# One unit for a differential head's context tiles, and the first latent leading products moved into the last head

## Chip, cores, metric

One Trainium2 chip, one of its cores. The metric is the device time of the whole program in microseconds (us).

## What is computed

Two layers over 1024 latent tokens and 256 context tokens of width 1024. The even layer projects the tokens and runs two groups of attention heads side by side; the odd layer runs an mLSTM and a neighbourhood attention. The change touches the attention of the even layer, for the latent tokens (keys: latent and context, 1280) and for the context tokens (keys: context alone, 256):

```python
def diff_attention(q1, q2, k1, k2, v, lam):
    def one(a, b_):
        s1 = jnp.einsum('bhqd,bhkd->bhqk', a, k1).astype(F32) * DA_SCALE
        s2 = jnp.einsum('bhqd,bhkd->bhqk', b_, k2).astype(F32) * DA_SCALE
        p = jax.nn.softmax(s1, axis=-1) - lam * jax.nn.softmax(s2, axis=-1)
        return jnp.einsum('bhqk,bhkd->bhqd', p.astype(v.dtype), v)
    return blocked_queries(one, q1, q2)

def softmax_attention(q, k, v, scale):
    def one(qb):
        s = jnp.einsum('bhqd,bhkd->bhqk', qb, k).astype(F32) * scale
        p = jax.nn.softmax(s, axis=-1).astype(v.dtype)
        return jnp.einsum('bhqk,bhkd->bhqd', p, v)
    return blocked_queries(one, q)
```

There are 4 differential heads (two maps each) and 8 latent (MLA) heads, which the kernel takes in 4 pairs. After the differential product comes an RMS norm and a gate.

## The kernel before

The program is a chain of stages: projections of layer 0, the attention stage, an output product with layer norm, and the same for layer 1. Only the attention stage is touched. It goes over four `Differential` units (the heads, `da`) and then four `Latent` units (the pairs, `mla`). A token tile is 128 queries: tiles 0 to 7 are latent tokens, 8 and 9 context tokens (`LT` is 8).

**A differential tile** (`Differential.plan`, line 554). For each of its two maps b, TensorE multiplies the queries with the keys' high and low parts into a score tile `s` of three PSUM banks (L565, L566; six matmuls for 1280 keys), VectorE takes the negated row maximum (`top`, L1227), ScalarE the exponential with its row sum (L1234), and then the score tile is free. VectorE combines the two maps with a ratio (L579, L580, L585), TensorE turns the result in groups of four (L1251), ScalarE and VectorE copy it out of PSUM (L518), TensorE multiplies it with the values (L596). ScalarE keeps the product (L600) and sums its squares (L605). After tiles 3, 7 and 9, `finish` (L629) normalizes, turns (L655), gates (L660) and stores (L665) a group of tiles.

There are **two score tiles** (`s`, 2 x 3 banks) and two turning tiles (`tp`, one bank each), which is all of PSUM. A map of a context tile has 256 keys only, and takes a score tile, a maximum and an exponential of its own all the same.

**A latent pair** works on blocks of keys by queries, with the keys in the partitions, in three one-bank tiles `st` (L760 to L762). So that its exponentials need no maximum in that layout, each query's shift is made beforehand: `Latent.shifts` (L702) gives a list of steps, one for each head a of the pair and each tile i of a group of four (or two) query tiles. A step is a rough score product in an `s` tile (L713) and its negated maximum (`nmx`, L721); after a group's last step the maxima are turned into a row (L729) and put beneath the queries (L734). A pair has three groups: tiles 0 to 3, tiles 4 to 7 (eight steps each) and the context tiles 8 and 9 (four steps). While one group's blocks run, the steps of the next group are interleaved with them.

**Order.** The instructions' order on each engine is fixed when the program is built. `Plan.add` (L428 ff.) lists tasks with an engine, an estimated cost, what they come after and which buffers they take and give. `Plan.run` (L463) looks at the first 99 tasks that are left, and emits the one that could start first by those estimates, with a small correction for each kind of task. Each engine then works through its instructions strictly in that order; a waiting instruction holds up all behind it. The main loop lists, for each head, the tiles in the order 0, 1, 2, 8, 3, 4, 9, 5, 6, 7, and the loads of the next head (`loaded`, which come into the place of the head before this one) at tile 4. After the last head it lists the eight steps of the first latent group, and then a task `banks`, which takes both score tiles at once, gives one back and makes the three `st` tiles out of the other's banks. Latent blocks can only follow `banks`.

## Time and profile before

| | |
|---|---|
| three runs | 1952.52, 1952.61, 1955.57 us (median 1952.61) |
| the profiled execution | 1954.08 us, span 1952.4 us, mean granted TensorE clock 0.966 |
| busy, share of the span | TensorE (PE) 93%, weight loads (PEld) 77%, VectorE (DVE) 57%, ScalarE (ACT) 37%, GpSimd (POOL) 27% |
| differential heads | from 460 us to 708.7 us |
| latent pairs | first block at 743.3 us, to about 1035 us |

The profile comes from one execution, times are from the start of its span. TensorE's busy time is that of pipelined matmuls whose ends are modelled, and TensorE's sequencer pairs each matmul with a weight load; an fp32 product shows as two matmuls. PEclk is the clock that was granted, as a share of full speed. A wait is put down to what ended it.

### The profile page before, as it was taken

To read this page: it belongs to the slowest core of one execution; us is meant where nothing else is said; L and a number is where in the kernel's file an instruction comes from. 1 tells how busy PE (TensorE), PEld (TensorE's weight loads), DVE (VectorE), ACT (ScalarE), POOL (GpSimd) and SP (SyncE) were. 2 spreads that over 40 slices of the span, in tenths; PEclk is the share of its full clock that TensorE was granted. 3 is DMA by queue.
4 is the path that set the end of the run, shared out by engine and by line. 5 is a ranking of instruction groups with operands and counts; after the bars stand their busy time and mean duration, and the time that the engine had idled before them with its cause. 6 is when DMAs were issued, how large, how long until landed. Compare 5 with 4: busy or idle time off the path is not lost.

```text
span 1952.4 us, 29575 instructions
## 1 busy us (share of the span) xinstructions
PE 1807.2 (93%) x11069; PEld 1508.0 (77%) x11069; DVE 1118.1 (57%) x2155; ACT 722.3 (37%) x1432; POOL 527.4 (27%) x542
## 2 busy tenths in 40 slices
PE   7999999999888889898899989999998998998898
PEld 5898998887777775555556779888898877877686
DVE  3654124314878887656666864665776324666756
ACT  2311014434665554343452312233553224444521
POOL 1433233100102212354463431220111002223444
PEclk9999999999989998898899999999999999999999
DMA  9756424677534644504016333224543366676652
GB/s 281 236 202 219 159 75 127 191 204 187 128 76 115 170 100 135 128 6 116 25 60 213 130 108 117 73 83 159 162 128 93 101 187 177 163 206 188 177 162 86
DMA packets 241588, 275.95 MB, mean 141 GB/s; under 512 B 25042, under 2 KB 201118, under 8 KB 241446
## 3 DMA queue, kind: packets, MB, share of 16 engines
q1 hardware_dynamic: 241446, 274.07, 48.6%
q8 instruction: 87, 1.43, 0.3%
q14 instruction: 55, 0.45, 0.1%
HBM read 193.14 MB, written 87.16 MB: 144 GB/s over the span
## 4 chain that ended last, share of the span: by engine, by line
PE 59%; DVE 13%; DMA 4%; issue 2%; ACT 2%; POOL 1%; SPq 1%; DVEq 0%; POOLq 0%; ACTq 0%
PE mm L390 6%; PE mm L392 6%; PE mm L391 6%; PE tp L796 4%; PE tp L596 3%; DVE nm L1227 3%; PE mm L1876 3%; PE mm L1877 2%; PE mm L1878 2%; PE st L760 2%; PE st L762 2%; PE st L761 2%; PE s L713 2%; DVE nmx L721 2%; PE tp L2309 2%
## 5 line engine op out<-in xcount | busy, mean ns | idle before, releaser
L347 POOL TENSOR_TENSOR wlo<-raw,whi 128x1024 fp32r<-128x1024 f32 (+2 forms) x39 | 94.4, 2420 | 227.2 <-ACT whi L339 223.9
L390 PE MATMUL mm<-whi,hhi 128*128 128x256 f32 (+1 forms) x496 | 147.8, 298 | 0.0
L392 PE MATMUL mm<-whi,hlo 128*128 128x256 f32 (+1 forms) x496 | 146.9, 296 | 0.2 <-DVE hlo L290 0.2
L391 PE MATMUL mm<-wlo,hhi 128*128 128x256 f32 (+1 forms) x496 | 146.6, 296 | 0.0
L1227 DVE TENSOR_REDUCE nm<-s 128x1 f32<-128x1280 f32 (+1 forms) x80 | 100.8, 1274 | 59.1 <-PE s L566 58.1
L339 ACT CAST whi<-raw 128x1024 fp32r<-128x1024 f32 (+2 forms) x54 | 56.0, 1036 | 180.8 <-DMA raw<-in_ev_w_in_dram 71.2
L721 DVE TENSOR_REDUCE nmx<-s 128x1 f32<-128x1280 f32 (+1 forms) x80 | 100.6, 1271 | 38.6 <-PE s L713 38.3
L2266 POOL TENSOR_SCALAR np<-np,nrz 128x640 f32<-128x640 f32 x64 | 53.0, 831 | 232.3 <-DVE nrz L2263 211.3
L565 PE MATMUL s<-o 128*128 128x512 f32 (+1 forms) x208 | 85.5, 417 | 27.4 <-ACT p L1234 27.1
L1234 ACT ACTIVATE p<-s,nm 128x1280 f32<-128x1280 f32 (+1 forms) x80 | 92.6, 1158 | 39.1 <-DVE nm L1227 31.4
L390 PEld LDWEIGHTS mm<-whi,hhi 128*128 128x128 f32 x496 | 94.8, 191 | 2.1 <-issue 1.7
L392 PEld LDWEIGHTS mm<-whi,hlo 128*128 128x128 f32 x496 | 94.8, 191 | 0.5 <-DVE hlo L290 0.4
L391 PEld LDWEIGHTS mm<-wlo,hhi 128*128 128x128 f32 x496 | 94.9, 191 | 0.2
L596 PE MATMUL tp<-v,pt 128*128 128x128 f32 x672 | 82.0, 280 | 0.3
L596 PEld LDWEIGHTS tp<-v,pt 128*128 128x128 f32 x672 | 80.4, 196 | 2.2 <-ACT pt L518 1.0
L1876 PE MATMUL mm<-h,whi 128*128 128x512 f32 x192 | 78.9, 411 | 3.3 <-DVE hv L1912 3.3
L713 PE MATMUL s<-o 96*128 96x512 f32 (+1 forms) x208 | 64.0, 410 | 17.0 <-DVE nmx L721 15.7
L776 ACT ACTIVATE pt<-st 128x512 f32<-128x512 f32 (+1 forms) x88 | 50.8, 578 | 72.3 <-PE st L762 67.8
L1877 PE MATMUL mm<-h,whi 128*128 128x512 f32 x192 | 76.3, 397 | 0.0
L1878 PE MATMUL mm<-h,wlo 128*128 128x512 f32 x192 | 76.1, 396 | 0.0
L644 POOL TENSOR_TENSOR rs<-rs,mhalf 128x4 f32<-128x4 f32 (+1 forms) x12 | 11.0, 914 | 239.8 <-DVE rs L640 239.8
L566 PE MATMUL s<-o 128*128 128x512 f32 (+1 forms) x208 | 74.2, 368 | 0.0
(470 smaller groups left out, 5390.8 us busy)
## 6 DMA issues: line engine op xcount, KB each, us to landing
adaw<-in_ada_w_dram SPq DMA_DIRECT2D x16, 1024.0 KB
raw<-in_od_w_in_dram SPq DMA_DIRECT2D x32, 512.0 KB
o<-s_qk SPq DMA_DIRECT2D x48, 320.0 KB
raw<-in_ev_w_in_dram SPq DMA_DIRECT2D x18, 512.0 KB
bt<-s_bt SPq DMA_DIRECT2D x16, 576.0 KB
adaw<-in_ada_w_dram SPq DMA_DIRECT2D x16, 512.0 KB
o<-s_mq SPq DMA_DIRECT2D x16, 480.0 KB
s_gate<-e SPq DMA_DIRECT2D x24, 256.0 KB
```

Of the source, the lines that this page charges most:

```text
L347: (eng or self.eng).tensor_tensor(out=lo, in0=self.raw, in1=hi, op=ALU.subtract)
L390: T.matmul(ps, ahi(k), bhi(k), start=k == k0, stop=False)
L391: T.matmul(ps, ahi(k), blo(k), start=False, stop=False)
L392: T.matmul(ps, alo(k), bhi(k), start=False, stop=k == nk - 1)
L596: T.matmul(o[:, :P], x["pt"][:, c, :], self.v[:, k0 + c, :], start=c == 0, stop=c == nch - 1)
L713: T.matmul(x["s", a, i][:, n0:n0 + nn], self.qh[a][0:96, (t0 + i) * P:(t0 + i + 1) * P], self.kh[a][0:96, k0 * P + n0:k0 * P + n0 + nn], s ...
L721: V.tensor_reduce(out=x["m", a][:, i:i + 1], in_=x["s", a, i][:, :w], axis=AX.X, op=ALU.max, negate=True)
L1227: V.tensor_reduce(out=nm, in_=s[:, :w], axis=AX.X, op=ALU.max, negate=True)
L1234: S.activation(out=p[:, :w], in_=s[:, :w], func=AF.Exp, bias=nm, accum_out=z)
L1876: T.matmul(ps, ah, bh, start=k == 0, stop=False)
L1877: T.matmul(ps, ah, bl, start=False, stop=False)
L1878: T.matmul(ps, al, bh, start=False, stop=k == KT - 1)
```

## The change

For each head the two context tiles become one unit, `plan_context`: the products of both tiles and both maps lie side by side in one score tile (4 x 256 columns), with one reduction over all four, four exponentials out of it into two buffers, one pair of ratio instructions, two combinations, one turn of four and one pair of value products in one turning tile. The order of the tiles becomes 0, 1, 2, context, 3 to 7, and the next head's loads are listed at tile 0. `Latent.shifts` does the same for a pair's context group: its four products form one step with one score tile and one reduction. In the last head, the steps of the first latent group are listed among its tiles, one after each.

```diff
--- before.py
+++ after.py
@@ -626,6 +626,82 @@
                 if tt == t0 + n - 1:
                     self.finish(t0, n, last)
 
+        def plan_context(self):
+
+            k0, w, t0 = LT, NCTX, LT
+            x = {}
+
+            def cut(b):
+                def emit(_):
+                    if b == 0:
+                        x["s"] = taken("s")
+                    for i in range(2):
+                        ql = self.q[b][:, (t0 + i) * P:(t0 + i + 1) * P]
+                        cs = slice((2 * b + i) * w, (2 * b + i + 1) * w)
+                        ks = slice(k0 * P, k0 * P + w)
+                        T.matmul(x["s"][:, cs], ql, self.kh[b][:, ks], start=True, stop=False)
+                        T.matmul(x["s"][:, cs], ql, self.kl[b][:, ks], start=False, stop=True)
+                return emit
+
+            def top(_):
+                x["m"] = at.tile([P, 4], F32, name="nmx", bufs=4)
+                V.tensor_reduce(out=x["m"], in_=x["s"][:, :4 * w].rearrange("p (m k) -> p m k", k=w), axis=AX.X,
+                                op=ALU.max, negate=True)
+
+            def exps(b):
+                def emit(_):
+                    x["p", b] = taken("p")
+                    if b:
+                        x["z"] = at.tile([P, 2], F32, name="zc", bufs=2)
+                    for i in range(2):
+                        m = 2 * b + i
+                        S.activation(out=x["p", b][:, i * w:(i + 1) * w], in_=x["s"][:, m * w:(m + 1) * w], func=AF.Exp,
+                                     bias=x["m"][:, m:m + 1],
+                                     accum_out=x["z"][:, i:i + 1] if b else self.r1[:, t0 + i:t0 + i + 1])
+                    if b:
+                        given("s", x["s"])
+                return emit
+
+            def scale(_):
+                x["ratio"] = ratio = at.tile([P, 2], F32, name="ratioc", bufs=2)
+                V.reciprocal(out=ratio, in_=x["z"])
+                V.scalar_tensor_tensor(out=ratio, in0=ratio, scalar=nlam, in1=self.r1[:, t0:t0 + 2], op0=ALU.mult, op1=ALU.mult)
+
+            def combine(_):
+                for i in range(2):
+                    p1, p2 = [x["p", b][:, i * w:(i + 1) * w] for b in range(2)]
+                    V.scalar_tensor_tensor(out=p1, in0=p2, scalar=x["ratio"][:, i:i + 1], in1=p1, op0=ALU.mult, op1=ALU.add)
+                given("p", x["p", 1])
+
+            ...
+
+            a = plan.add("P", 0.48, cut(0), [self.ready[0]], ["s"])
+            a = plan.add("P", 0.48, cut(1), [a, self.ready[1]])
+            a = plan.add("V", on_vector(4 * w), top, [a], rank=RANK)
+            a = plan.add("A", 1.1, exps(0), [a], ["p"], rank=RANK)
+            a = plan.add("A", 1.1, exps(1), [a], ["p"], ["s"], rank=RANK)
+            a = plan.add("V", 0.33, scale, [a])
+            a = plan.add("V", 0.8, combine, [a], [], ["p"])
+            ...
+            self.finish(t0, 2, a)
+
         def finish(self, t0, n, last):
 
             x = {}
@@ -734,6 +810,32 @@
                 return emit
+
+            def together(_):
+                x["s"] = taken("s")
+                for a in range(2):
+                    for i in range(n):
+                        cs = slice((n * a + i) * w, (n * a + i + 1) * w)
+                        T.matmul(x["s"][:, cs], self.qh[a][0:96, (t0 + i) * P:(t0 + i + 1) * P],
+                                 self.kh[a][0:96, k0 * P:k0 * P + w], start=True, stop=True)
+
+            def tops(_):
+                m = at.tile([P, 4], F32, name="nmx", bufs=4)
+                V.tensor_reduce(out=m, in_=x["s"][:, :4 * w].rearrange("p (m k) -> p m k", k=w), axis=AX.X, op=ALU.max,
+                                negate=True)
+                given("s", x["s"])
+                for a in range(2):
+                    x["m", a] = m[:, n * a:n * a + n]
+
+            def context():
+                last = plan.add("P", 0.48, together, [*self.ready[:2]], ["s"])
+                last = plan.add("V", on_vector(4 * w), tops, [last], [], ["s"])
+                for a in range(2):
+                    t = plan.add("P", 0.2, turn(a), [last], ["tp"])
+                    self.shift[g, a] = plan.add("A", on_scalar(n * P, False), row(a), [t], [], ["tp"])
+
+            if n * w <= 512:
+                return [context]
 
             def step(a, i):
                 last = None
@@ -1339,12 +1441,21 @@
 
         loaded(da[1])
         for u in da:
-            for tt in (0, 1, 2, 8, 3, 4, 9, 5, 6, 7):
-                if tt == 4 and u.h:
+            for tt in (0, 1, 2, LT, 3, 4, 5, 6, 7):
+                if tt == 0 and u.h:
                     loaded(units[u.h + 1])
                 first = len(plan.tasks)
-                u.plan(tt)
+                if tt == LT:
+                    u.plan_context()
+                else:
+                    u.plan(tt)
                 plan.tasks[first].emit = stepped(plan.tasks[first].emit)
+                if u.h == 3:
+                    if tt == 0:
+                        ahead = mla[0].shifts(plan, 0)
+                    for step in ahead[:1 if tt < 7 else None]:
+                        step()
+                    ahead = ahead[1:]
         last_scores = [x for x in plan.tasks if x.eng == "P" and "k11" in x.give][-1]
         done = [plan.tasks[-1]]
 
@@ -1360,8 +1471,6 @@
                 given("st", single.tile([P, 512], F32, name=f"st{i}"))
 
         groups = [(u, g) for u in mla for g in range(len(TG))]
-        for step in groups[0][0].shifts(plan, 0):
-            step()
         plan.add("P", 0.01, banks, [last_scores], ["s"] * 2, ["s"] + ["st"] * 3)
         spread(plan, w1.begin(), done)
         for i, (u, g) in enumerate(groups):
```

What that does to the order on the engines, at three places. Line numbers move: L713 and L721 become L789 and L797, L729 becomes L805, L760 to L762 become L862 to L864, L1251 becomes L1353, L1227 becomes L1329, L1234 becomes L1336.

**The seam between the heads and the pairs, on TensorE.** Before, the last rough products ahead of the first latent block (`s` are the score tiles, `o_...` the loaded queries and keys of the pair's two heads, `st` the block's tile):

```order
L713 MATMUL s_4838<-o_6598 128x512 x2
L713 MATMUL s_4838<-o_6598 128x256
L713 MATMUL s_4856<-o_6598 128x512 x2
L713 MATMUL s_4856<-o_6598 128x256
L713 MATMUL s_4838<-o_6598 128x512 x2
L713 MATMUL s_4838<-o_6598 128x256
L713 MATMUL s_4856<-o_6590 128x256
L729 MATMUL tp_4839<-cst,nmx 1x128 x4
L713 MATMUL s_4838<-o_6590 128x256
L713 MATMUL s_4856<-o_6598 128x256
L729 MATMUL tp_4840<-cst,nmx 1x128 x2
L760 MATMUL st_7213<-o_6590 128x512
```

And now, the rows around the first latent block:

```order
L789 MATMUL s_4838<-o_6431 128x512 x2
L789 MATMUL s_4838<-o_6431 128x256
L789 MATMUL s_4856<-o_6431 128x512 x2
L789 MATMUL s_4856<-o_6431 128x256
L805 MATMUL tp_4839<-cst,nmx 1x128 x4
L862 MATMUL st_7096<-o_6366 128x512
L863 MATMUL st_7096<-o_6366 128x512
L864 MATMUL st_7096<-o_6366 128x512
L1353 MATMUL tp_4840<-cst,p_4843 128x128 x4
L1353 MATMUL tp_4839<-cst,p_4843 128x128 x2
L862 MATMUL st_7097<-o_6431 128x512
L863 MATMUL st_7097<-o_6431 128x512
```

Before, all twenty steps of the first pair's three groups stood between the last head's score products and the first block, and the head's turns and values stood among them. Now eight stand there, those of the second group; transposes of the head's last tiles (L1353, and after these rows L596 for two tiles) stand behind the block, and the context group's step comes later.

**The last head, on VectorE**, behind its context unit (`nmx_6543`, `nmx_6745` and `nmx_6806` are the maxima of the first latent group; the numbers are those of the buffers):

```order
L518 COPY pt0_4846<-tp0_4839 128x256
L797 TENSOR_REDUCE nmx_6745<-s1_4856 128x1
L797 TENSOR_REDUCE nmx_6745<-s0_4838 128x1
L797 TENSOR_REDUCE nmx_6745<-s1_4856 128x1
L797 TENSOR_REDUCE nmx_6745<-s0_4838 128x1
L1329 TENSOR_REDUCE nm_6779<-s1_4856 128x1
L1329 TENSOR_REDUCE nm_6792<-s0_4838 128x1
L736 SCALAR_TENSOR_TENSOR yd_6795<-tp1_4840,subgt_96,gt_5668 128x512
L797 TENSOR_REDUCE nmx_6806<-s1_4856 128x1
L579 RECIPROCAL ratio_6812<-zs_6798 128x1
L580 SCALAR_TENSOR_TENSOR ratio_6812<-ratio_6812,r1_6463,nlam_90 128x1
L1329 TENSOR_REDUCE nm_6817<-s0_4838 128x1
```

Twelve reductions L797 stand in this head: four into `nmx_6543` for the pair's first head, four into `nmx_6745` and four more into `nmx_6806`, both for its second head. Before, none stood there.

**A context tile, on ScalarE**, in the third head. Before, the first of its two context tiles:

```order
L1234 ACTIVATE p_4843,r_5907<-s_4838,nm 128x1280
L1234 ACTIVATE p_4842,zs<-s_4856,nm 128x1280
L1234 ACTIVATE p_4845,r_5907<-s_4838,nm 128x256
L518 COPY pt_4847<-tp_4839 128x256
L518 COPY pt_4847<-tp_4840 128x256 x2
L1234 ACTIVATE p_4844,zs<-s_4856,nm 128x256
L1234 ACTIVATE p_4841,r_5907<-s_4838,nm 128x1280
L518 COPY pt_4848<-tp_4839 128x256
```

And now the unit for both:

```order
L518 COPY pt_4850<-tp_4840 128x256 x2
L518 COPY pt_4850<-tp_4839 128x256 x2
L658 ACTIVATE p_4841,r_5911<-s_4838,nmx 128x256 x2
L658 ACTIVATE p_4844,zc<-s_4838,nmx 128x256 x2
L518 COPY pt_4846<-tp_4839 128x256
L1336 ACTIVATE p_4843,r_5911<-s_4856,nm 128x1280
L600 COPY oo<-tp_4840 128x128
L518 COPY pt_4846<-tp_4839 128x256
```

The four exponentials of a tile pair stood in two places, each behind a maximum of its own and with maps of other tiles between; now the four (two rows marked x2) follow one another, out of one score tile.

## Rows read from the trace of the kernel before

**Rows 1.** Windows: length, busy us PE, PEld, DVE, ACT, POOL; PEclk, DMA, GB/s.

```profile
642.00:708.70 66.70, 57.67 (x380) 50.09 (x378) 53.67 (x98) 40.93 (x102) 10.32 (x19) 0.95 0.48 127
708.70:727.80 19.10, 16.61 (x111) 14.87 (x112) 16.61 (x28) 7.56 (x22) 2.78 (x5) 0.91 0.87 208
727.80:743.30 15.50, 10.60 (x44) 5.78 (x42) 15.15 (x14) 1.72 (x3) 0.00 (x0) 0.90 0.50 135
```

**Rows 2.** Waits from 460 to 730 us: total us, times, longest.

```profile
PEld s L565 <- ACT p L1234: 33.0, 27, 2.1
ACT p L1234 <- DVE nm L1227: 31.4, 31, 1.9
```

**Rows 3.** Groups of instructions by form, 514 to 708.7 us.

```profile
L1227 DVE TENSOR_REDUCE nm<-s 128x1 f32<-128x1280 f32 x48 | 70.6, 1486 | 12.3 <-PE s L566 11.9 <-PE tp L1251 0.2
L1234 ACT ACTIVATE p<-s,nm 128x1280 f32<-128x1280 f32 x49 | 65.1, 1329 | 29.9 <-DVE nm L1227 23.3 <-DVE p L585 3.5 <-PE tp L1251 2.5
...
L585 DVE SCALAR_TENSOR_TENSOR p<-p,ratio,p 128x256 f32<-128x256 f32 x30 | 14.1, 477 | 0.0
...
L1234 ACT ACTIVATE p<-s,nm 128x256 f32<-128x256 f32 x12 | 5.7, 474 | 0.0
L1227 DVE TENSOR_REDUCE nm<-s 128x1 f32<-128x256 f32 x12 | 5.1, 423 | 2.0 <-PE s L566 1.7
```

**Rows 4.** Timeline of VectorE, third differential head: start, us, instruction, idle before.

```profile
600.49 2.89 DVE L1227 TENSOR_REDUCE nm<-s 128x1 f32<-128x1280 f32 x2 [0.16 <-PE s L566]
...
621.42 2.89 DVE L1227 TENSOR_REDUCE nm<-s 128x1 f32<-128x1280 f32 x2 [0.67 <-PE s L566]
...
628.02 1.49 DVE L1227 TENSOR_REDUCE nm<-s 128x1 f32<-128x1280 f32 x1
...
637.46 2.89 DVE L1227 TENSOR_REDUCE nm<-s 128x1 f32<-128x1280 f32 x2 [0.63 <-PE s L566]
...
642.24 1.48 DVE L1227 TENSOR_REDUCE nm<-s 128x1 f32<-128x1280 f32 x1
```

**Rows 5.** Windows of 4 us: columns as in rows 1.

```profile
608.00:612.00 4.00, 2.69 (x12) 2.22 (x12) 3.60 (x6) 1.49 (x5) 0.52 (x1) 0.70 0.20 78
740.00:744.00 4.00, 3.34 (x11) 1.80 (x12) 3.44 (x9) 0.93 (x2) 0.00 (x0) 0.51 0.00 0
744.00:748.00 4.00, 4.00 (x11) 3.13 (x10) 0.05 (x1) 1.63 (x3) 2.64 (x6) 0.50 0.01 2
```

**Rows 6.** Timeline of VectorE at the seam between the stages.

```profile
708.75 1.48 DVE L1227 TENSOR_REDUCE nm<-s 128x1 f32<-128x1280 f32 x1
710.15 0.15 DVE L579 RECIPROCAL ratio<-zs 128x1 f32<-128x1 f32 x1
710.34 0.22 DVE L580 SCALAR_TENSOR_TENSOR ratio<-ratio,r,nlam 128x1 f32<-128x1 f32 x1
...
712.60 0.74 DVE L585 SCALAR_TENSOR_TENSOR p<-p,ratio,p 128x512 f32<-128x512 f32 x1
...
727.24 0.48 DVE L660 SCALAR_TENSOR_TENSOR yd<-tp,subgt,gt 128x256 f32<-128x256 f32 x1 [0.20 <-ACT oo L600]
727.76 14.40 DVE L721 TENSOR_REDUCE nmx<-s 128x1 f32<-128x1280 f32 x11
```

**Rows 7.** Timeline of TensorE at the same seam.

```profile
718.96 1.09 PE L1251 MATMUL tp<-cst,p 128*128 128x128 f32 x8
...
724.53 2.40 PE L596 MATMUL tp<-v,pt 128*128 128x128 f32 x20
...
734.89 0.84 PE L713 MATMUL s<-o 96*128 96x512 f32 x3 [0.55 <-DVE nmx L721]
...
743.32 0.79 PE L760 MATMUL st<-o 96*128 96x512 f32 x1
```

**Rows 8.** Timeline of SyncE's queue: first and last of twelve latent loads.

```profile
641.90 0.33 SPq L691 DMA_DIRECT2D o<-s_mq  x1
...
650.61 0.30 SPq L693 DMA_DIRECT2D o<-s_kr  x1
```

17 lines of the change are left out of this document (added).

## Prediction

> **What bounds the kernel now.** I read the windows by stage first. From 460 to 708.7 us the differential heads run, and no engine is full: in the last head's 66.7 us TensorE is busy for 57.7 and VectorE for 53.7 [rows 1]. The chain of waits says what couples them: TensorE waits for an exponential on ScalarE to free a score tile, and ScalarE for VectorE's maximum [rows 2]. Two score tiles circulate, TensorE to VectorE to ScalarE and back. Where no context tile lies between, maps start 14.22 us for four apart (628.02 to 642.24), 3.56 each (rows marked x2 hold two maps) [rows 4], though the reduction takes 1.49 and the exponential less [rows 3].
>
> Two places are worse. First the context tiles: from 600.49 to 621.42 four intervals take 20.93 us, with one context tile among them, and from 621.42 to 637.46 they take 16.04, with the other [rows 4]. Against 14.22 that is 6.7 and 1.8, so 8.5 us a head. In the first of the two stretches the granted clock is 0.70 [rows 5]. Second the seam to the latent heads: the last differential map's reduction starts at 708.75 [rows 6], the first `st` product only at 743.32 [rows 7]. In those 34.6 us VectorE makes twenty `nmx` reductions, and from 727.8 on it is the bound: 15.15 of 15.5 us busy, TensorE 10.60 [rows 1]. The eleven in the row at 727.76 take 14.40 us, ten at 1.40 and a short one [rows 6]. All twenty run ahead of the `banks` task, since that wants both score tiles at once.
>
> **The change part by part.** The sum is made against the profiled execution, 1954.1 us, whose span is 1952.4; the median of the runs is 1952.6, 1.5 below.
>
> *Context tiles.* Each head had two, with four small maps that each took a score tile, a reduction of 0.42 us and an exponential of 0.47 [rows 3]; they are one unit now, in one tile, with one reduction of 1024. Between 0.42 for 256 and 1.49 for 1280 elements [rows 3] that is 1.22 us by a straight line, against 1.7 for the four: of itself almost nothing. What may go is the second stretch of coupling. The new unit costs at least its VectorE work, about 3 us (1.22, two combinations of 0.48 [rows 3], some small ones and a copy), and at most what the dearer context tile costs now, 6.7. I take 5.5, near the upper end, because the tile is held through one reduction and four exponentials in a row, some 4 us. Saved: 3 us a head, **-12** for four (bounds -22 and -7).
>
> *Latent products in the last head.* Here the change does more than its words. The step list is cut with `ahead[:1 if tt < 7 else None]`, and LT is 8: at the context unit all five steps that are left are issued, while the list loses one. So the four maps of the second latent head are issued again at tiles 3 to 6. The order bears this out: `nmx_6745` and `nmx_6806` are filled four times each for the same head, and twelve `L797` reductions stand in this head, not eight. Four are sheer addition. Each of the twelve is a product of three matmuls (0.84 us busy [rows 7]) and a reduction with a pace of 1.40. Lower bound: all of VectorE's idle 13.0 us in this head [rows 1] takes them in, and 12 x 1.40 - 13.0 = 4 is left. Upper bound: each pushes the next map by a whole interval, 12 x 3.56 = 43. I take 1.5 each, **+18**: nearest is the 1.40 of the stretch in which VectorE alone paced them [rows 6], and the order puts four in a block with no map between, as there; of the rest part fits into gaps, but they use the tiles that the maps wait for.
>
> *The seam.* Behind the last map's reduction VectorE now has the context's gating (0.48), two ratio pairs (0.15 + 0.22 each), one combination of 0.74 and eight reductions at 1.40 [rows 6]: with the last map's own 1.48 some 14.6 us, and 0.4 for the turn of the maxima. 34.6 becomes 15, **-19** (bounds -20 and -17, if VectorE must wait in between). The context group's products, four of the twenty, went behind `banks` and became one; they cost TensorE the same columns, and I put this at nothing: latent blocks on TensorE hide the reduction. Without that cover it would be 1.2 us a latent pair.
>
> *What the seam hid.* Before, the tail of the last head (turns and values) ran under those reductions. Now sixteen transposes, the values of two tiles and a turn of four lie behind the first `st` product, where TensorE is the bound: 16 x 0.136, 2 x 2.40 and 0.5 [rows 7] make 7.5 us. VectorE's share of the tail is covered by TensorE there. Against it, TensorE ran the first 8 us of that stage at a clock of 0.51 and 0.50 [rows 5], its lower level of 1.2 GHz, after a stretch in which it was idle for 4.9 of 15.5 us; that cost 4 us at full clock. The new stretch is shorter and has transposes in it, so I count half back: **+5.5** (bounds +2 and +8). The Trainium skill's page "TensorE: Matmul & The Clock Gate", Part 1, What's actually happening, says that the default state is throttled and activity releases it. The trace agrees with the fall (0.51). By that rule alone the eight paced products idle the engine just as much, nothing comes back, and the sum below would be -5.5; by the row alone, with all 4 us back, -9.5.
>
> *Edits at nothing.* The loads of the next head are listed at tile 0 instead of tile 4, but SyncE's order leaves the latent loads right behind the stores of the third head, and they were already issued when its last maps had released the tiles (641.90 to 650.61 [rows 8]). They now have a reader within the head. Between the last product that frees the first tile and that reader TensorE has thirty transposes at 0.136 and the values of three tiles at 2.40 [rows 7], 11.3 us before the three maps are counted, and the issue takes 8.7; if this cover failed, the stall would be up to 8.7. On SyncE's queue stands the context store of the third head, whose gating on VectorE is long done by then. The bias tables advance by nine steps a head in place of ten, so a few of their stores come later, under the latent heads.
>
> Sum: -12 + 18 - 19 + 5.5 = **-7.5**. That gives 1946.6 for the profiled execution and 1952.6 - 7.5 = 1945.1 for the median.
>
> **Rivals.**
> 1. *The score tiles price the twelve products (slower).* The place is the last head, tiles 0 to 7. A latent product takes a turn in the circulation as a map does (3.56 us [rows 4]), without the exponential's leg of 1.33 [rows 3]: 2.2 to 3.56 us each, and I put 2.6. It decides from (12 + 19 - 5.5) / 12 = 2.1 us each. For it: the waits named in [rows 2], and four products that are pure repetition. Against: 13 us of idle VectorE [rows 1]. Time: 31 in place of 18, +5.7, so 1958.
> 2. *The merged context unit saves little.* Everything in it hangs on one reduction, and one tile is out of circulation for 4 us. At 7.5 us a head the saving is 1 each, -4: sum +0.5, 1953. For it: the cheaper context tile costs but 1.8 now [rows 4]. Against: the clock of 0.70 and the doubled stretch.
> 3. *The gaps swallow the products.* At the lower bound, +4: sum -21.5, 1931. For it: idle time [rows 1]. Against: four come in a block.
> 4. *The latent loads come late.* A stall of some 4 us ahead of the first `L789`: 1949. Against: the count of work above.
>
> **How the numbers follow.** A measurement of this kernel can tell about 0.2%, 3.9 us, from no change. The forecast has 0.50, rival 3 has 0.12: faster 0.62. Rival 2 has 0.17 and rival 4 0.04: same 0.21. Rival 1: slower 0.17. The forecast's own range, with 1.2 to 1.8 us a product and 2 to 4 us a head, is 1937 to 1953. The range over the cases, from rival 3's end to rival 1's, is 1932 to 1958; corners beyond it (both bounds at once) are left out.
>
> **What would show it.** Right: the first `st` product 15 to 17 us behind the last differential reduction; twelve reductions of `L797` in the last head, which is about 15 us longer than the one before; heads two and three some 3 us shorter; a latent stage longer by some 5 us to its first values. Wrong: maps in the last head apart by more than 5 us on average; heads as long as before in spite of one context unit; a wait of TensorE for a DMA at the first `L789`; or idle VectorE in the seam.

## The result, and the profile after

The changed kernel takes **1938.11 us** (median of 4 runs, 1937.53 to 1943.08), the kernel before 1953.34 beside it: a ratio of 0.9926, 95% interval 0.9907 to 0.9945, so 14.5 us less (10.7 to 18.2). The prediction was 1945.1 and its range 1932 to 1958; the time lies at the lower end of the forecast's own range, 1937 to 1953. The gain is about twice the 7.5 us that were worked out, and the terms missed by more than the total: three by 5 to 11 us each, partly in opposite directions.

First the windows of the kernel before, by head and the seam (from one first reduction of a head to the next, then to the first `st` product; columns as in [rows 1]):

```profile
461.60:516.49 54.89, 45.66 (x281) 38.83 (x280) 43.53 (x71) 36.54 (x85) 2.64 (x6) 0.94 0.63 137
516.49:581.96 65.47, 56.55 (x366) 49.30 (x365) 51.62 (x95) 39.40 (x99) 6.87 (x16) 0.92 0.50 107
581.96:646.85 64.89, 54.47 (x367) 46.86 (x366) 53.79 (x96) 39.60 (x99) 14.39 (x22) 0.97 0.50 118
646.85:708.75 61.90, 54.05 (x359) 47.30 (x358) 48.91 (x91) 38.06 (x97) 10.32 (x20) 0.94 0.44 119
708.75:743.32 34.57, 27.23 (x154) 20.66 (x154) 31.73 (x41) 9.23 (x25) 2.77 (x5) 0.90 0.71 175
```

and the same stages of the changed kernel:

```profile
460.52:512.96 52.44, 45.97 (x289) 38.57 (x287) 43.29 (x66) 37.95 (x89) 1.63 (x4) 0.93 0.66 143
512.96:570.49 57.53, 51.70 (x367) 45.33 (x367) 48.74 (x84) 41.40 (x105) 6.87 (x16) 1.00 0.59 136
570.49:628.83 58.34, 51.63 (x367) 45.28 (x367) 50.14 (x84) 41.44 (x105) 13.90 (x22) 1.00 0.57 127
628.83:706.05 77.22, 66.21 (x419) 56.79 (x420) 62.52 (x89) 42.25 (x107) 10.44 (x19) 0.93 0.32 79
706.05:722.25 16.20, 11.93 (x37) 7.91 (x37) 14.85 (x16) 2.64 (x5) 1.16 (x1) 0.53 1.02 219
```

The second and third heads are 7.9 and 6.6 us shorter, and TensorE runs at its full clock in them (1.00, before 0.92 and 0.97). The last head is 15.3 us longer, the seam 18.4 us shorter. The first `st` product comes 21.1 us earlier (743.32 to 722.25), the end only 15.5 (span 1952.4 to 1936.9).

The waits of the changed kernel from 460 to 722 us that answer to [rows 2], then its groups by form from 513 to 706 us, which answer to [rows 3]:

```profile
PEld s L565 <- ACT p L1336: 20.0, 16, 2.1
ACT p L1336 <- DVE nm L1329: 30.9, 30, 3.0
```

```profile
L1329 DVE TENSOR_REDUCE nm<-s 128x1 f32<-128x1280 f32 x47 | 69.5, 1489 | 7.6 <-PE s L566 6.3
L797 DVE TENSOR_REDUCE nmx<-s 128x1 f32<-128x1280 f32 x12 | 17.6, 1483 | 1.0 <-PE s L789 1.0
L648 DVE TENSOR_REDUCE nmx<-s 128x4 f32<-128x1024 f32 x3 | 3.7, 1218 | 1.4 <-PE s L643 1.4
L658 ACT ACTIVATE p<-s,nmx 128x256 f32<-128x256 f32 x12 | 5.5, 474 | 0.2
```

TensorE waits for the maps' score tiles 16 times in this row and not 27. The big maps cost each what they did (1.49 us), the reduction of 1024 takes the 1.22 that a straight line gave, and the four exponentials 0.47 each. So these instructions cost what they did; the work between them moved closer. VectorE also has less to do: 84 instructions in each of the second and third heads in place of 95 and 96, and 2.9 and 3.7 us less busy time. Most of that is seven copies out of PSUM a head (L518, 0.42 us each), which the new order gives to ScalarE (35 there and 7 on VectorE, before 28 and 14); no run keeps them where they were, so their share in the gain is not shown. Twelve L797 reductions stand in the last head, as counted.

The third head on VectorE, to be read against [rows 4]:

```profile
586.64 1.49 DVE L1329 TENSOR_REDUCE nm<-s 128x1 f32<-128x1280 f32 x1
588.47 1.49 DVE L1329 TENSOR_REDUCE nm<-s 128x1 f32<-128x1280 f32 x1 [0.34 <-PE s L566]
592.05 1.21 DVE L648 TENSOR_REDUCE nmx<-s 128x4 f32<-128x1024 f32 x1
594.29 1.48 DVE L1329 TENSOR_REDUCE nm<-s 128x1 f32<-128x1280 f32 x1
600.08 1.49 DVE L1329 TENSOR_REDUCE nm<-s 128x1 f32<-128x1280 f32 x1
605.25 3.10 DVE L1329 TENSOR_REDUCE nm<-s 128x1 f32<-128x1280 f32 x2 [0.18 <-PE s L566]
610.43 2.89 DVE L1329 TENSOR_REDUCE nm<-s 128x1 f32<-128x1280 f32 x2 [0.25 <-PE s L566]
616.32 1.49 DVE L1329 TENSOR_REDUCE nm<-s 128x1 f32<-128x1280 f32 x1
```

From 586.64 to 605.25 four intervals with the unit take 18.61 us. The four behind them, to 616.32, take 11.07: **2.77 a map, where the prediction took 3.56 as the undisturbed pace.** The trace of before had that pace too, two rows behind the ones quoted in [rows 4]:

```profile
642.24 1.48 DVE L1227 TENSOR_REDUCE nm<-s 128x1 f32<-128x1280 f32 x1
644.07 1.48 DVE L1227 TENSOR_REDUCE nm<-s 128x1 f32<-128x1280 f32 x1
646.85 1.48 DVE L1227 TENSOR_REDUCE nm<-s 128x1 f32<-128x1280 f32 x1
```

From 637.46 [rows 4] to 646.85 four intervals take 9.39 us, 2.35 each. But the maps come unevenly, and four intervals are a short stretch: the twelve intervals of the changed kernel's third head that are not those with the unit average 3.31 us ((58.34 - 18.61) / 12).

The seam on VectorE, which answers to [rows 6], and on TensorE, which answers to [rows 7]:

```profile
706.05 1.49 DVE L1329 TENSOR_REDUCE nm<-s 128x1 f32<-128x1280 f32 x1 [1.63 <-PE s L566]
...
711.32 5.91 DVE L797 TENSOR_REDUCE nmx<-s 128x1 f32<-128x1280 f32 x4 [0.55 <-PE s L789]
717.66 4.51 DVE L797 TENSOR_REDUCE nmx<-s 128x1 f32<-128x1280 f32 x3 [0.43 <-PE s L789]
```

```profile
722.25 0.78 PE L862 MATMUL st<-o 96*128 96x512 f32 x1
...
730.07 2.40 PE L596 MATMUL tp<-v,pt 128*128 128x128 f32 x20
...
733.43 2.40 PE L596 MATMUL tp<-v,pt 128*128 128x128 f32 x20
```

VectorE is busy for 14.85 of the 16.2 us, eight reductions in a row, and the values of two tiles now lie behind the first `st` product, as the prediction said. TensorE's clock there, in windows of 4 us that answer to [rows 5]:

```profile
718.20:722.20 4.00, 2.60 (x8) 1.22 (x7) 3.87 (x4) 0.00 (x0) 0.00 (x0) 0.50 1.01 217
722.20:726.20 4.00, 3.98 (x13) 3.35 (x14) 3.26 (x8) 1.91 (x4) 0.00 (x0) 0.50 0.85 247
726.20:730.20 4.00, 4.00 (x22) 3.18 (x21) 2.00 (x7) 2.62 (x6) 2.82 (x6) 0.82 0.27 69
```

It is near its lower level, 1.2 GHz, through the whole seam (0.53 in the mean of 16.2 us) and for some microseconds behind it; before, the seam ran at 0.90 and only its end and the first blocks at 0.51 and 0.50 [rows 5]. The latent loads on SyncE's queue, first and last, which answer to [rows 8]:

```profile
621.00 0.32 SPq L767 DMA_DIRECT2D o<-s_mq  x1
...
631.12 0.30 SPq L769 DMA_DIRECT2D o<-s_kr  x1
```

They are issued 20 us earlier, and nobody waits for them at the first L789. The first latent values follow the first `st` product by 17.7 us, before by 12.2: the 5 us that the prediction named as a sign. One of its signs of being wrong came too, just: the maps of the last head stand 77.2 / 15 = 5.1 us apart.

### The profile page after: what moved, and what is told of

Same layout as the page of the kernel before. It is cut to its first block, busy times and chain, and to the rows that moved or that the text cites. A ratio compares the mean times of both kernels' runs of the same rounds, so it can differ in the third digit from the quotient of the medians.

```text
span 1936.9 us, 29600 instructions
## 1 busy us (share of the span) xinstructions
PE 1803.0 (93%) x11085; PEld 1504.4 (78%) x11085; DVE 1128.5 (58%) x2116; ACT 728.3 (38%) x1451; POOL 513.1 (26%) x531
## 4 chain that ended last, share of the span: by engine, by line
PE 59%; DVE 11%; DMA 5%; issue 3%; ACT 3%; POOL 1%; SPq 1%; DVEq 0%; POOLq 0%; ACTq 0%
PE mm L390 6%; PE mm L392 6%; PE mm L391 6%; PE tp L898 4%; PE tp L596 3%; PE mm L1985 3%; PE mm L1986 2%; PE mm L1987 2%; PE st L862 2%; PE st L864 2%; PE st L863 2%; PE s L789 2%; PE tp L1353 2%; DVE nm L1329 2%; PE s L565 2%
## 5 line engine op out<-in xcount | busy, mean ns | idle before, releaser
L1329 DVE TENSOR_REDUCE nm<-s 128x1 f32<-128x1280 f32 x64 | 94.6, 1489 | 53.0 <-PE s L566 51.5
L797 DVE TENSOR_REDUCE nmx<-s 128x1 f32<-128x1280 f32 x68 | 100.5, 1485 | 37.0 <-PE s L789 36.5
L1336 ACT ACTIVATE p<-s,nm 128x1280 f32<-128x1280 f32 x64 | 85.0, 1329 | 35.4 <-DVE nm L1329 30.9
L565 PE MATMUL s<-o 128*128 128x512 f32 (+1 forms) x192 | 79.8, 420 | 18.1 <-ACT p L1336 16.4
L390 PEld LDWEIGHTS mm<-whi,hhi 128*128 128x128 f32 x496 | 94.7, 191 | 2.1 <-issue 1.7
L391 PEld LDWEIGHTS mm<-wlo,hhi 128*128 128x128 f32 x496 | 94.7, 191 | 0.2
L789 PE MATMUL s<-o 96*128 96x512 f32 (+1 forms) x204 | 65.4, 430 | 17.8 <-DVE nmx L797 11.2
L878 ACT ACTIVATE pt<-st 128x512 f32<-128x512 f32 (+1 forms) x88 | 50.7, 578 | 75.1 <-PE st L864 70.9
L596 PE MATMUL tp<-v,pt 128*128 128x128 f32 x640 | 76.8, 276 | 0.7 <-ACT pt L518 0.2
L596 PEld LDWEIGHTS tp<-v,pt 128*128 128x128 f32 x640 | 74.4, 192 | 3.7 <-DVE pt L518 2.4
L2368 ACT ACTIVATE np<-np,nnm 128x640 f32<-128x640 f32 x64 | 52.9, 827 | 56.4 <-DVE nnm L2362 51.0
L862 PE MATMUL st<-o 96*128 96x512 f32 (+1 forms) x176 | 73.1, 415 | 0.0
```

The costliest lines, as they stand in the source:

```text
L390: T.matmul(ps, ahi(k), bhi(k), start=k == k0, stop=False)
L391: T.matmul(ps, ahi(k), blo(k), start=False, stop=False)
L565: T.matmul(s[:, n0:n0 + nn], ql, self.kh[b][:, ks], start=True, stop=False)
L596: T.matmul(o[:, :P], x["pt"][:, c, :], self.v[:, k0 + c, :], start=c == 0, stop=c == nch - 1)
L789: T.matmul(x["s", a, i][:, n0:n0 + nn], self.qh[a][0:96, (t0 + i) * P:(t0 + i + 1) * P], self.kh[a][0:96, k0 * P + n0:k0 * P + n0 + nn], s ...
L797: V.tensor_reduce(out=x["m", a][:, i:i + 1], in_=x["s", a, i][:, :w], axis=AX.X, op=ALU.max, negate=True)
```

## The experiments

Each run is split here into its stages: the four heads, the seam, the first pair (from its first `st` product to that of the second pair), the pairs two to four (to the first output product), and the rest. Every number is a difference of two starts in that run's trace (the rest goes to the end of the span). It is one trace of each run: the first head with the unit has the same order of instructions in nine runs and takes 50.7 to 53.6 us there, at a clock of 1.00 down to 0.93.

| run | heads 1 to 4 | seam | first pair | pairs 2 to 4 | rest | median us |
|---|---|---|---|---|---|---|
| before | 54.9 65.5 64.9 61.9 | 34.6 | 72.6 | 218.4 | 918.0 | 1953.3 |
| after | 52.4 57.5 58.3 77.2 | 16.2 | 74.3 | 217.4 | 922.9 | 1938.1 |
| e1 context unit only | 52.5 57.5 59.1 55.2 | 33.0 | 69.7 | 220.3 | 921.3 | 1932.5 |
| e2 two tiles | 54.9 64.6 64.9 83.4 | 10.5 | 69.9 | 219.0 | 917.0 | 1947.9 |
| e3 adjacent | 53.9 61.6 61.7 79.1 | 14.9 | 73.8 | 218.4 | 919.0 | 1941.7 |
| e4 no repeat | 50.7 57.5 58.3 74.0 | 16.2 | 74.3 | 217.4 | 922.9 | 1936.0 |
| e5 steps behind | 51.8 57.5 59.8 55.2 | 33.9 | 63.2 | 217.9 | 916.9 | 1921.3 |
| e6 hold behind | 50.7 57.5 58.4 55.2 | 19.8 | 73.5 | 219.0 | 922.6 | 1922.3 |
| e7 hold in head | 53.6 59.0 58.3 73.0 | 4.7 | 77.9 | 218.8 | 919.9 | 1928.2 |
| e8 filler | 56.0 65.5 66.9 62.9 | 36.5 | 73.0 | 220.7 | 923.0 | 1965.2 |
| e9 split latent | 50.7 57.5 58.4 76.0 | 16.0 | 75.9 | 220.4 | 916.2 | 1935.2 |
| e10 loads at 4 | 52.5 57.5 60.6 56.8 | 34.6 | 63.4 | 218.1 | 919.7 | 1925.2 |
| e11 latent unit only | 52.9 64.5 64.9 62.0 | 36.0 | 63.5 | 218.2 | 919.3 | 1946.2 |
| e12 hold half | 50.7 57.5 58.3 55.3 | 26.2 | 68.6 | 217.9 | 919.7 | 1921.7 |

The rest lies behind the change and still spreads from 916.2 to 923.0, though TensorE's instructions stand there in the same order in the changed kernel (922.9) and in e5 (916.9). Part of these 6 us goes with TensorE's clock: two stretches of the rest, the same matmuls in both runs, took 35.29 and 104.00 us at 0.90 and 0.93 in the changed kernel (from 1323.45 and 1776.53) and 33.88 and 102.15 at 0.95 and 0.97 in e5 (from 1308.46 and 1758.64), 3.3 us together. What sets the clock there, and the other 2.7 us, stays open; where a term is sized below, it is by the stages ahead of them.

**e1, the context unit alone**, in the kernel before:

```diff
-            for tt in (0, 1, 2, 8, 3, 4, 9, 5, 6, 7):
+            for tt in (0, 1, 2, LT, 3, 4, 5, 6, 7):
...
-                u.plan(tt)
+                if tt == LT:
+                    u.plan_context()
+                else:
+                    u.plan(tt)
```

> The kernel before with the merged context unit alone: loads stay at tile 4, the latent steps stay behind the last head. Theory M (the merge itself gives the time, about 7 us a head and 2.5 in the first): heads of 52, 57.5, 58 and 55 us, a seam of 34.6 as before, about 24 us faster than the kernel before, 1929 us. That would also mean that the other half of the change costs about 9 us. My forecast's price, 3 us a head: 12 us faster, 1941. Theory L (the gain comes from the loads at tile 0 and the new order of the queue, not from the merge): within 4 us of before, 1950 to 1955.

Ratio 0.9892 (0.9870 to 0.9914), 21 us less than before: theory M, and not the 12 of the forecast. The heads are those of the changed kernel, the last one 55.2. The four together lose 22.8 us. And e1 is faster than the whole change by the medians (1932.5 to 1938.1): something in the other half seems to cost time, though the two intervals overlap.

**e2, two context tiles again**, in the changed kernel, and **e3, both side by side**:

```diff
-            for tt in (0, 1, 2, LT, 3, 4, 5, 6, 7):
+            for tt in (0, 1, 2, 8, 3, 4, 9, 5, 6, 7):
...
-                if tt == LT:
-                    u.plan_context()
-                else:
-                    u.plan(tt)
+                u.plan(tt)
...
-                if u.h == 3:
+                if u.h == 3 and tt != 9:
```

(e3: `(0, 1, 2, 8, 9, 3, 4, 5, 6, 7)`.)

> The changed kernel with two context tiles of four small maps again, at their old places (behind tiles 2 and 4); loads and latent steps as changed. Theory M: about 24 us slower than the changed kernel, 1962, the second and third heads again 65 us long. My forecast's price of 3 us a head: 1950. Theory L: within 4 us of the changed kernel, 1934 to 1942.

> As the run with two tiles, but both context tiles stand side by side behind tile 2, so that the row of maps is broken once and not twice. If it is the number of breaks that costs (theory M1): at least half of the merge's gain is kept, at most 8 us above the changed kernel, 1946. If it is the four small maps, each of which takes a score tile of its own through three engines (theory M2): no gain against the two tiles at their old places, within 4 us of that run.

e2: ratio 0.9974 (0.9959 to 0.9989), e3: 0.9936 (0.9915 to 0.9956). In e2 the second and third heads are back at 64.6 and 64.9, with the loads at tile 0: theory L is out, and the gain in the heads is the merge's. The whole came out 14 us below M's 1962, because the seam (10.5), the first pair (69.9) and the rest (917.0) are shorter here than in the changed kernel. In e3 the two heads take 123.3 us together, 129.5 in e2 and 115.9 in the changed kernel:

```profile
515.87:577.45 61.58, 55.57 (x393) 49.66 (x391) 50.06 (x92) 43.93 (x119) 8.26 (x20) 0.97 0.53 107
577.45:639.13 61.68, 54.13 (x353) 45.51 (x352) 52.32 (x96) 40.29 (x101) 20.97 (x31) 0.97 0.52 123
```

So 6.2 of 13.6 us go with one break in the row of maps in place of two, and 7.4 with the four small maps in tiles of their own: about half each. M2 alone is out, and M1's "at least half" is met over all four heads (11.5 of 22.3 us) and just missed in these two. The last head keeps 4.3 of 6.2 us (79.1); there the two tiles aren't side by side, as latent products stand between them. In e3 most copies are already with ScalarE (7 and 8 a head left on VectorE), so the 7.4 us are not theirs; in the 6.2 they may have a part, and the clock in both.

**e4, each latent step once:** `ahead[:1 if tt < 7 else None]` becomes `ahead[:1 if tt != 7 else None]`.

> The changed kernel with each latent step of the last head issued once: eight L797 reductions in that head and not twelve. By my forecast's price of 1.5 us a product: 6 us faster, 1932, the last head 71 us long. If the merge gives 7 us in the last head too, the products cost (15.3 + 6.6) / 12 = 1.8 each: 7.3 us faster, 1931. If the gaps swallow them (4 us for all twelve): 1 to 2 us faster, 1936 to 1937. If each pushes a map by a whole turn of 3.56 us: 14 us faster, 1924.

Ratio 0.9910 (0.9889 to 0.9931), against 0.9926 no difference that the intervals tell apart. In the trace the last head is 74.0 and not 77.2: four products fewer save 3.2 us, 0.8 each, and the eight that stay cost 74.0 - 55.2 = 18.8, or 2.35 each. Forecast were 1.5 for all. By place, the four are the block behind the context unit (on VectorE four L797 in a row from 667.44 on in the changed kernel, none there in e4), and the eight stand one by one between maps, where the changed kernel has its other eight. The windows of its last head and of that of e5, which has no latent products there:

```profile
629.01:703.02 74.01, 64.45 (x403) 55.44 (x404) 56.87 (x86) 41.71 (x106) 10.43 (x19) 0.91 0.31 82
```

```profile
630.00:685.21 55.21, 49.36 (x352) 43.55 (x353) 46.80 (x81) 39.85 (x101) 10.56 (x20) 1.00 0.49 122
```

VectorE works 10.1 us more and TensorE 15.1, of it at least part by the clock (0.91 against 1.00). What the clock costs is read below, at e8.

**e5, the steps behind the last head**, with all else as changed, and **e10**, which puts the loads back to tile 4 as well:

```diff
-                if u.h == 3:
-                    if tt == 0:
-                        ahead = mla[0].shifts(plan, 0)
-                    for step in ahead[:1 if tt < 7 else None]:
-                        step()
-                    ahead = ahead[1:]
...
+        for step in groups[0][0].shifts(plan, 0):
+            step()
```

> The changed kernel with the latent steps of the first group behind the last head again, as before; the merged units, the merged latent context group and the loads at tile 0 stay. It differs from the run with the context unit alone (1932.5) only in the latent context group and the place of the loads. Theory A (of the other half of the change only the move of the products costs): within 3 us of that run, 1930 to 1935, last head 55 us, seam 28 to 33. Theory B (the loads or the merged latent context group cost the 5.6 us by which the changed kernel lies above that run): 1936 to 1940.

> The run with the steps behind (1921.3) with the loads of the next head at tile 4 again, so that it differs from the run with the context unit alone (1932.5) by the latent context unit and nothing else. If the latent unit makes those 11 us: 1919 to 1924. If the loads at tile 0 make them: 1930 to 1935. In between, both.

e5: ratio 0.9846 (0.9821 to 0.9871), 30 us less than before and 16.8 less than the changed kernel by the medians. Neither theory had it: moving the products into the last head costs 17 us by the medians and 13.7 by the start of the first output product (1000.3 and 1014.0), not 5.6. e10: 0.9857 (0.9840 to 0.9873), not told apart from e5, so the loads are worth nothing that shows; and by the medians 7 us below e1 (the two intervals just meet), from which it differs by the latent context unit alone. The seam and the first pair in e5, and then in the changed kernel:

```profile
685.21:719.14 33.93, 28.86 (x156) 21.41 (x155) 30.62 (x36) 8.36 (x25) 3.60 (x7) 0.82 0.61 150
719.14:782.37 63.23, 59.65 (x258) 36.45 (x257) 43.43 (x44) 28.30 (x49) 24.39 (x21) 0.93 0.50 136
```

```profile
722.25:796.57 74.32, 68.80 (x325) 44.55 (x326) 51.89 (x63) 31.48 (x61) 25.35 (x26) 0.91 0.56 159
```

The move brings 17.7 us in the seam and costs 22.0 in the last head and 11.1 in the first pair.

**e9 and e11, the latent context unit**: taken out of the changed kernel (the two lines `if n * w <= 512: return [context]`), and put alone into the kernel before.

> The changed kernel with the latent context group in four products and four reductions again; nothing else. Theory A (the latent context unit is worth what I forecast, nothing to 1 us a pair, since the latent blocks on TensorE cover its VectorE work): 1938 to 1941. Theory B (it is worth the 11 us that lie between the run with the context unit alone and the run with the steps behind): 1946 to 1950.

> The kernel before with the latent context unit alone (one product tile, one reduction per pair); the differential heads have their two context tiles, the steps lie behind the last head. Theory A: within 4 us of before, 1949 to 1953. Theory B, and the gain does not depend on the rest: 1940 to 1944. In the profile: first pair 66 us rather than 72.6 between its first st product and that of the second pair.

e11: ratio 0.9969 (0.9957 to 0.9981), 6 us less; its first pair takes 63.5 and not 72.6, the pairs two to four 218.2 and 218.4. e9: 0.9917 (0.9900 to 0.9934), not told apart from the changed kernel. So the unit is worth 6 to 9 us in the first pair where the products lie behind the last head (e10 and e11), 1.6 there in the changed kernel (e9), and up to 1 us in each later pair. The trace of before shows why; TensorE, then VectorE in the same stretch:

```profile
774.70 0.28 PE L713 MATMUL s<-o 96*128 96x256 f32 x1
...
782.19 0.37 PE L729 MATMUL tp<-cst,nmx 128*1 128x128 f32 x1 [2.90 <-DVE nmx L721]
782.21 0.78 PE L760 MATMUL st<-o 96*128 96x512 f32 x1
```

```profile
776.67 1.78 DVE L787 TENSOR_TENSOR oo<-p,pt 128x512 f32<-128x512 f32 x1
778.55 1.59 DVE L787 TENSOR_TENSOR oo<-oo,p 128x512 f32<-128x512 f32 x1
780.24 1.56 DVE L787 TENSOR_TENSOR oo<-oo,pt 128x512 f32<-128x512 f32 x1
781.72 0.41 DVE L721 TENSOR_REDUCE nmx<-s 128x1 f32<-128x256 f32 x1
```

The pair's last small context product ran at 774.70, its reduction stood behind other work on VectorE, three additions last, until 781.72, and TensorE stood 2.90 us in front of the turn of that maximum, with the next block behind it. The Trainium skill's page "PSUM — Partial Sum Buffer", section Engine vs sequencer instructions, says that VectorE's queue is strictly first in, first out and that matmuls start in program order; these rows agree, with 7 us between a product and a reduction of 0.41. The clock fell with it, and with the unit neither happens. Windows of the kernel before, and of e11 over the same group of blocks:

```profile
780.00:784.00 4.00, 1.81 (x6) 1.07 (x8) 3.79 (x5) 0.42 (x2) 2.84 (x2) 0.63 0.69 190
784.00:788.00 4.00, 4.00 (x10) 1.02 (x10) 0.27 (x1) 0.54 (x1) 1.26 (x1) 0.51 0.00 0
```

```profile
764.45:789.18 24.73, 24.73 (x108) 14.75 (x107) 19.32 (x19) 13.66 (x23) 12.04 (x7) 1.00 0.37 108
```

That group took 30.27 us before (765.69 to 795.96) and takes 24.73. The other 3.0 of the 9.1 us lie in the pair's third group: 20.0 us before, 17.0 in e11, e10 and e5. In these three runs three first products of the next pair stand in it, and one more in the second group; in all others four stand in the third, and TensorE waits a second time for VectorE, here in the kernel before:

```profile
811.64 1.44 PE L713 MATMUL s<-o 96*128 96x512 f32 x3 [1.58 <-DVE nmx L721]
```

**e6, e7, e12, products held behind the banks task**: the second group's steps and the context unit may start only behind it, in e5 (e6: all eight steps; e12: those of the second head) and in e4 (e7).

```diff
-                    last = plan.add("P", nn / 2250, rough(a, i, n0, nn), [last or self.ready[a]], ["s"] if n0 == 0 else [])
+                    last = plan.add("P", nn / 2250, rough(a, i, n0, nn), [last] if last else [self.ready[a], self.hold], ["s"] if n0 == 0 else [])
...
-        plan.add("P", 0.01, banks, [last_scores], ["s"] * 2, ["s"] + ["st"] * 3)
+        mla[0].hold = plan.add("P", 0.01, banks, [last_scores], ["s"] * 2, ["s"] + ["st"] * 3)
```

> As the run with the steps behind the last head, but the products of the second latent group (and the context group) may start only behind the banks task, so eight and not sixteen precede the first latent block. If the seam is VectorE's row of reductions: seam 14 to 17, first st product 15 us earlier. If the later products then hide under the latent blocks: 1916 to 1921. If what the seam hid comes back as it did in the changed kernel (5 us): 1921 to 1925. If the held products stall the blocks: over 1930.

> The changed kernel with each step issued once (1936.0) and the second group's products held behind the banks task, so that no latent product is left between the last differential map and the banks task: seam 3 to 5 in place of 16.2. With 8 of those 12 us lost again to the tail of the last head: 1932; with none lost: 1924. Against the run with the steps behind and held it shows the price of eight products in the last head (18.8 by the last run) against the same eight in a row (8 x 1.4 = 11.2): some 5 to 8 us slower than that run.

> As the run with the second group held behind the banks task (1922.3), but only the four products of its second latent head and the context unit are held; the first head's four run ahead of it. If a product costs 1.4 us in the seam and 0.65 us of TensorE under the blocks, and the tail of the last head is already covered by twelve: seam 25, first pair 67 to 70, 1917 to 1922. If holding anything costs the first pair 10 us: 1926 to 1930.

Ratios 0.9845 (0.9825 to 0.9865), 0.9868 (0.9848 to 0.9888) and 0.9845 (0.9827 to 0.9863). Seam and first pair together take 97.2 us in e5, 94.7 in e12, 93.3 in e6, 82.6 in e7, whose last head is 18 us longer. The seam shrinks as the row of reductions does (33.9, 26.2, 19.8, 4.7), and the first pair grows by half to three quarters of that (63.2, 68.6, 73.5, 77.9). e6 and e12 can't be told from e5. e5, e6 and e12 beat both kernels, by 1.5% against before and 0.8% against the changed kernel.

**e8, TensorE kept busy in the context tiles** of the kernel before:

```diff
+                    if tt >= LT:
+                        for _ in range(4):
+                            T.matmul(s[:, 512:1024], ql, self.kh[b][:, 0:512], start=True, stop=True)
```

> The kernel before with its two context tiles, and behind each of the four small maps of a context tile pair four more matmuls of 512 columns into columns of the score tile that nobody reads (work that isn't needed, about 1 us a map, 4 us a head, in stretches where TensorE was idle). Theory C (about half of the merge's gain in the second and third head is TensorE's clock, which falls to 0.6 to 0.7 behind each context tile): the clock stays near 1.0 and the second and third heads are 1 to 4 us shorter, 1944 to 1951. Theory H (the tiles' hand-over costs, the clock is only seen beside it): the clock may rise but heads are as long or up to 4 us longer, 1952 to 1968.

Ratio 1.0046 (1.0025 to 1.0066). In its second head the clock rose from 0.92 to 0.97 and the head took 65.5 us, as before; the third kept 0.97 and took 66.9 in place of 64.9:

```profile
517.64:583.18 65.54, 57.51 (x382) 49.36 (x381) 51.28 (x95) 39.56 (x99) 6.88 (x16) 0.97 0.50 108
583.18:650.03 66.85, 57.73 (x383) 49.34 (x382) 52.94 (x96) 39.83 (x99) 14.45 (x22) 0.97 0.48 113
```

Theory C's 1 to 4 us did not come. As the filler costs time itself and lifted the clock only part of the way, this does not exclude that the clock has a share in the merge's gain. The other traces show one. The second head of e7 has the same order of instructions on TensorE, VectorE and ScalarE as that of the changed kernel (57.53 us at 1.00), and ran at 0.97:

```profile
515.18:574.19 59.01, 53.17 (x367) 46.81 (x367) 48.72 (x84) 41.31 (x105) 6.88 (x16) 0.97 0.56 131
```

The second head in the order of the kernel before took 65.47 us at 0.92 there, and 64.52 at 0.95 in e11. So 0.03 of the clock goes with 1.0 to 1.5 us of such a head. By an estimate from these rows some 3 to 4 of the second head's 7.9 us, and 1.0 to 1.5 of the third's 6.6, came with the clock, and the rest did not. Why it falls in some heads of one order and not in others isn't shown.

## Why the prediction was right in its range and wrong in its parts

**Context tiles: forecast -12, found -22.8** (between -17 and -25 with the other traces of the same heads). This term was mis-sized, about at its bound of -22. The step that failed first is the base: "Against 14.22 that is 6.7 and 1.8". The 14.22 us were themselves behind a context tile, and 9.44 of them (628.02 to 637.46) stand in the 16.04 as well. Against the 2.77 a map of the changed kernel, the two stretches of [rows 4] cost 20.93 + 16.04 - 22.1 = 14.8 us a head, and the unit costs 18.61 - 11.07 = 7.5, so 7.3 is saved, where the second and third heads show 7.9 and 6.6. Against the 3.31 of the twelve other intervals they cost 10.5 and 5.4, and 5.1 is saved. So what the unit removed was dearer than the 8.5 that I took, by either base; whether the unit costs my 5.5 or rival 2's 7.5 depends on the base. The mechanism, one break of the circulation and not two, held for about half: e3 keeps 6.2 of 13.6 us with one break. The other half goes with the four small maps in tiles of their own, where I had put "of itself almost nothing"; the busy time that they took is indeed small, but not what they delayed. Part of either half is the clock, and how much of the first is the copies that moved to ScalarE is open.

**Twelve products: forecast +18, found +22.0** (77.2 in the changed kernel, 55.2 in e1 and e5; 76.0 for the same order in e9, where the clock was 0.96 and not 0.93). Inside the bounds, near rival 1's deciding price of 2.1 in the mean (1.8). But the spread was misjudged: the eight that stand one by one between maps cost 2.35 each, the four in a block 0.8. The comparison "nearest is the 1.40 of the stretch in which VectorE alone paced them" was too dear for the block and too cheap for the others. "About 15 us longer than the one before" was met (77.2 against 61.9) by two misses against each other: 22.0 for the products, 6.7 for the last head's own merge, where 18 and 3 were forecast. (The 66.7 us that the prediction calls the last head's begin 4.85 us ahead of it, at 642.00; in the head's own 61.9 us VectorE idles for the same 13.0.)

**The seam: forecast -19 to 15 us, found -18.4 to 16.2**, VectorE busy for 14.85 of it. Right.

**What the seam hid: forecast +5.5 (+2 to +8), found +11.1**, the first pair of e5 against the changed kernel (63.2 to 74.3). The step counted the tail, 7.5 us, and half of the clock's 4 us back. The first of the pair's groups is indeed 6.8 us longer (21.5 in e5, 28.3 now). What the step left out: the second and third groups are longer too, by 1.7 and 2.6. The context unit, which stood ahead of the blocks in e5, now stands in the second, where TensorE waits 0.79 us for its turn, and the third has four first products of the next pair in place of three. Of the clock little came back: the first group ran at 0.84 for 22.4 us before and runs at 0.90 for 28.3 now, which is 3.6 and 2.8 us at full clock. The Trainium skill's page "TensorE: Matmul & The Clock Gate", Part 1, What's actually happening, whose rule the prediction set against the row, was the better guide: 0.53 in a seam of paced products, 0.50 for some 4 us behind it. The same page, A second HAM failure mode: psum-queue depth-cycling, describes, for a bf16 kernel, a clock that swings where TensorE idles between groups while it goes round through PSUM's banks; the heads of before agree (0.92 and 0.97). The changed kernel's second and third heads do not fall (1.00), but heads of their order ran at 0.97 in e5, e7 and e10.

**Latent context unit: forecast 0, found -9 in the first pair of the kernel before (e11), -6 behind the context unit (e1 to e10, 69.7 to 63.4).** Two steps failed. "All twenty run ahead of the banks task" was wrong, and so is the same count in the section on the change: nineteen did, and the twentieth stood among the blocks. And "latent blocks on TensorE hide the reduction" was wrong, as the turn of that maximum stood in TensorE's own queue ahead of the blocks. For the pairs two to four nothing was about right (0.2 less in e11, 3.0 in the changed kernel against e9, for three pairs).

**The rest, loads and bias tables: nothing forecast.** The loads brought and cost nothing that shows (e5 and e10). The give-back from the first `st` product to the end was 5.6 us, as the 5.5 forecast, but by accident: the first pair gave back 1.7 (11.1 less the 9.4 that the units took), the later pairs -1.0, and 4.9 lie in the rest, which differs by as much between runs with the same order of TensorE's instructions.

Along the chain from before over e1 and e5 to the changed kernel the stages ahead of the output add up: context tiles in the heads -22.8, products +22.0, the move in the seam -17.7, in the first pair +11.1, and the first pair's gains on the way -2.9 and -6.5 make -16.8; the smaller differences of the other stages and of the start (-1.1) bring it to the -20.4 by which the first output product is earlier. The forecast's errors were -10.8, +4, +0.6, +5.6 and -9: their sum, about -10, is near the 7 us by which it missed. That the time lies inside the range is in part luck: the misses were 20 us one way and 10 the other. The move itself, which gave the change half of its name, is a loss: 22.0 + 11.1 - 17.7 = 15 us, where the forecast had 18 - 19 + 5.5 = 4.5.

The rivals: loads late (4) and no gain from the unit (2) did not occur; rival 1's mechanism did, at 1.8 a product in place of 2.6, and was outweighed by the merge; rival 3's gaps took in part of the block of four alone (0.8 us each in place of 1.40).

## What to carry to other kernels

The pace against which a disturbance is priced must come from a stretch that the disturbance doesn't reach, else its price stands in the base as well. In an uneven loop a short stretch gives almost any pace (2.35, 2.77 and 3.56 us a map here, each from four intervals): take whole heads, or several stretches, before a difference is taken, and give the price with each base. Work put into a loop of circulating buffers costs what it delays there, not its own length: the same eight products cost 17.7 us between the maps (last head of e7 against e6) and 15.1 in a row behind them (seam of e6 against e7), where they also covered the tail (first pair 4.4 us shorter). A small reduction that "runs beside" TensorE is only hidden if nothing in TensorE's own queue waits for it.

## What was not expected of the hardware

Four more matmuls of 512 columns in each small map added 1.0 and 3.3 us to TensorE's busy time in the second and third heads and lengthened them by 0.1 and 2.0, although TensorE was idle there for 8.9 and 10.4 us. And the stage behind the change, with the same order of instructions on TensorE, took 916.9 us in one kernel and 922.9 in another, about half of it in two stretches in which the granted clock differed (0.90 and 0.93 against 0.95 and 0.97); why it differed, no trace tells.
